# First weight unit and a norm row moved to the ACT queue, gate biases fetched once a branch, last rows finished by DVE in halves

## The chip, the cores and the metric

The kernel runs on one core of a Trainium2 chip. The metric is the device time of one execution in microseconds (us), the median of several runs. Five engines work side by side, each through its own list of instructions in order: TensorE (PE, matmuls and transposes), VectorE (DVE), ScalarE (ACT), GpSimd (POOL) and SyncE (SP), which here only issues transfers. They wait for each other, and for transfers, through semaphores. Data lies in HBM, in the on-chip memory SBUF (128 partitions) and, as results of PE, in PSUM.

## What is computed

Two layers of a hybrid block, then one layer of a second kind, over 256 tokens of width 1024, all in float32. Cut to the parts that the change touches:

```
def hybrid_layer(x, mem, ...):                      # twice
    h = rms_norm(x, ln_mix);  z = h @ w_in          # w_in: 1024 x 6440
    k, v = split(rms_norm(mem, mem_norm) @ mem_w_kv)   # memory attention's keys and values
    ...                                             # three attention branches o_nsa, o_gla, o_mem
    gates = sigmoid(merge.reshape(B, S, 3, D) + b_merge)   # merge: the last 3072 columns of z
    merged = sum(gates[:, :, i] * (o_i @ w_branch[i]))
    x = x + merged @ w_out
    h = rms_norm(x, ln_mlp)
    return x + square(relu(h @ w_up)) @ w_down
...
def hybrid_layer_2(x, ...):                         # once, the end of the program
    ...
    out = mixed @ w_out
    return layer_norm(ALPHA * x + out, ln_g, ln_b)  # (y - mean) * rsqrt(var + eps) * g + b
```

## The kernel before, in words

**Numbers.** Every float32 factor is split into a high part and the rest (`hi` and `lo` for weights, `b8x`, `hh`/`hl`, `oh`/`ol` for activations), and each product is three matmuls (`mm3`, line 188 records them all): high by high, rest by high, high by rest.

**Weights.** `unit` (line 434) loads 128 x 1024 elements (512 KB) into one of four buffers `raw` by a transfer of SP, ACT (every sixth time POOL) rounds them to `hi` (line 431, or 429 on POOL), and DVE takes the difference `lo` (line 432). The next transfer into a buffer waits until its `lo` is done. The very first unit is `fine`: its two halves of 128 x 512 are loaded and split each by itself (lines 442, 444, 445).

**The start.** PE first multiplies zeros (`warm`, line 324). SP loads the identity matrix (`CF`), the left half of the memory's 256 rows (`gate`, two tiles of 128 rows, by 512 columns), the row of `mem_norm` (into `ROWA`, called `gtmp` in the trace), the first half unit of `mem_w_kv`, and the right half of the memory. PE turns `ROWA` (line 192), DVE copies the column (`COL`), PE turns the memory's chunks of 128 columns, and ACT and DVE scale them into `b8x` high and rest (lines 524, 525). The keys' product follows (8 chunks k by 2 tiles of tokens), then the values' product, into which the turning of `X` is woven (4 transposes of a psm buffer each, three buffers), then layer 0. The rows of `ln_mix` and `ln_mlp` are loaded into other rows of the same `ROWA`; so that load waits for the first turning.

**Order of work.** PE's order is the order of the code. The others' lists are ordered by the scheduler of the framework, which follows dependencies. SP and ACT are in order: a transfer behind a waiting one is not issued. Transfers are counted on eight semaphores in turn, so the ninth transfer of a row waits until the first has landed, and so on.

**Gate biases.** `gates_of` (line 1120) makes the gates of a branch: a broadcast of 1024 numbers of `b_merge` to all partitions, twice (one copy for each tile of tokens, 1024 KB), fetched by POOL's queue into the buffer `gate`, then for each half of 512 columns DVE's `acc * rstd + bias` (line 1129) and ACT's tanh. For the first branch the buffer is free as soon as the memory's rows are used up.

**The end.** `fin` (line 1622) takes the last product: the last tile of tokens is computed in quarters of 256 columns, DVE adds the residual and gathers statistics; then the mean and variance (`bmv`, 1633), on POOL variance + eps (`bve`, 1635) and the power -0.5 (`brs`, 1637), on DVE the centering (1640) in pieces of 256 and 768 columns; then 256 columns are scaled by ACT (1644) and shifted by POOL (1645), 768 are done by DVE in one operation (1647), and SP writes the two pieces out (1648), the one of 256 first.

Of the kernel before, what the change touches and what calls it, by code (L numbers as in the profile page):

```python
# [19 lines left out]
P = 128  # L20
# [8 lines left out]
WARM = 8  # L29
WARM2 = 8  # L30
NRAW = 4
# [67 lines left out]
def block_kernel(ctx, tc, x_in, mem_in, positions, ln_mix, w_in, b_merge, nsa_q_norm, nsa_k_norm,  # L99
# [22 lines left out]
    def nm(s):  # L122
        cnt[0] += 1
        return f"{s}_{cnt[0]}"
# [113 lines left out]

    def load_mem(parts=(0, 1), mid=None, m=None):
        if m is None:  # L240
            m = B8("gate", shape=(2, 1024))
        for hf in parts:
            for tt in range(2):
                hs = slice(512 * hf, 512 * hf + 512)
                nc.sync.dma_start(m[:, tt, hs], mem_in[0, tt * P:(tt + 1) * P, hs])
            if mid is not None:
                mid()
        return m
# [9 lines left out]

    def first_rows():
        nc.sync.dma_start(ROWA[32:48, :], mem_norm.rearrange("l (k p) -> (l k) p", p=P))  # L260

    def ln_rows():
        nc.sync.dma_start(ROWA[0:16, :], ln_mix.rearrange("l (k p) -> (l k) p", p=P))
        nc.sync.dma_start(ROWA[16:32, :], ln_mlp.rearrange("l (k p) -> (l k) p", p=P))

    MEM0 = load_mem((0,), first_rows)

    def load_x():
        mem_stats()
        for tt in range(2):  # L270
            nc.sync.dma_start(X[:, tt], x_in[0, tt * P:(tt + 1) * P, :])
# [55 lines left out]
    pt = PS()  # L327
    tr(pt[:, :128], ROWA, IDF)
    dve.tensor_copy(COL[:, 32:48], pt[:, 32:48])
# [104 lines left out]
    def unit(srcs, a, n, fine=False):  # L434
        raw = wraw.tile([P, 1024], F32, tag="raw", name=nm("raw"))
        hi = whl.tile([P, 1024], FR, tag="hi", name=nm("hi"))
        lo = whl.tile([P, 1024], FR, tag="lo", name=nm("lo"))
        rv = raw[:, :a * n].rearrange("p (a n) -> p a n", a=a)
        if fine:
            (pp, c0, c1, src), = srcs  # L440
            for j in range(a):
                nc.sync.dma_start(rv[:, j], src[:, j])
                js = slice(j * n, j * n + n)
                act(hi[:, js], raw[:, js], AF.Copy)  # L444
                dve.tensor_tensor(lo[:, js], raw[:, js], f32(hi[:, js]), op=OP.subtract)
                if j == 0 and fine is not True:
                    fine()
            return (hi[:, :a * n].rearrange("p (a n) -> p a n", a=a),
                    lo[:, :a * n].rearrange("p (a n) -> p a n", a=a))
        for pp, c0, c1, src in srcs:  # L450
            nc.sync.dma_start(rv[pp, :, c0:c1], src)
        split(hi[:, :a * n], lo[:, :a * n], raw[:, :a * n])
        return (hi[:, :a * n].rearrange("p (a n) -> p a n", a=a),
                lo[:, :a * n].rearrange("p (a n) -> p a n", a=a))

    def units(w2d, r0, nk, cols, paired=None, fine=False):
# [14 lines left out]
        while k < nk:  # L471
            a = min(per, nk - k)
            rs = w2d[r0 + k * P:r0 + (k + a) * P, :]
            srcs = []
            o = 0
            for c0, c1 in cols:
                srcs.append((slice(0, P), o, o + c1 - c0, rs[:, c0:c1].rearrange("(a p) n -> p a n", p=P)))
                o += c1 - c0
            h, lo = unit(srcs, a, n, fine)
            fine = fine if fine is True and k < 2 else False  # L480
            for j in range(a):
                res.append((h[:, j, :], lo[:, j, :]))
            k += a
# [118 lines left out]
    def mem_kv(l, mh, ml, mid=None):  # L602
        w = mem_w_kv[l]
        pk = tok_major(mh, ml, w, 0, 8, [(0, 512)], l == 0 and (lambda: (load_mem((1,), None, MEM0), ln_rows())))
        if mid is not None:
# [513 lines left out]

    def gates_of(l, b, hh, hl, rsd):  # L1120
        g = B8("gate", shape=(2, 1024))
        nc.gpsimd.dma_start(g, wrap(b_merge[l, b], [[0, P], [0, 2], [1, 1024]]))
        for h in range(2):
            hs = slice(512 * h, 512 * h + 512)
            c0 = 3368 + 1024 * b + 512 * h
            ps = tok_major(hh, hl, w_in[l], 0, 8, [(c0, c0 + 512)])
            for tt in range(2):
                gs = g[:, tt, hs]
                dve.scalar_tensor_tensor(gs, ps[tt], rsd[:, tt:tt + 1], gs, op0=OP.mult, op1=OP.add)
                act(gs, gs, AF.Tanh, scale=0.5)  # L1130
# [71 lines left out]
    def layer(l, hT):  # L1202
# [85 lines left out]
        for b in (2, 1, 0):  # L1288
            g = gates_of(l, b, hh, hl, rsd)
            if b == 2:  # L1290
# [100 lines left out]
    def layer_2(hT):  # L1391
# [229 lines left out]
        def fin(tt, h, ps):  # L1621
# [12 lines left out]
            ve = SM([P, 1], "bve")  # L1634
            pool.tensor_scalar(ve, mv[:, 1:2], LN_EPS, None, op0=OP.add)
            rs = SM([P, 1], "brs")
            pool.tensor_tensor(rs, ve, MH[:, 0:1], op=OP.pow)  # L1637
            cuts = (slice(0, 256), slice(256, 1024))
            for qs in cuts:
                dve.scalar_tensor_tensor(X[:, tt, qs], X[:, tt, qs], mv[:, 0:1], LG[:, 0, qs],  # L1640
                                         op0=OP.subtract, op1=OP.mult)
            for q, qs in enumerate(cuts):
                if q == 0:
                    act(X[:, tt, qs], X[:, tt, qs], AF.Copy, scale=rs)
                    pool.tensor_tensor(X[:, tt, qs], X[:, tt, qs], LG[:, 1, qs], op=OP.add)
                else:
                    dve.scalar_tensor_tensor(X[:, tt, qs], X[:, tt, qs], rs, LG[:, 1, qs], op0=OP.mult, op1=OP.add)
                nc.sync.dma_start(out[0, tt * P:(tt + 1) * P, qs], X[:, tt, qs])
# [47 lines left out]
```

## Time and profile before

| | us |
|---|---|
| median of 3 runs (1228.67, 1231.71, 1232.16) | 1231.71 |
| the profiled execution | 1227.59 |
| its span, first to last instruction | 1225.8 |
| PE busy in the span | 1200.9 (98%) |
| DVE, ACT, POOL busy | 852.6, 583.1, 213.7 |

A busy share is the time in which an engine had an instruction in hand; PE's weight loads run beside its matmuls and have a row of their own. The 1.8 us between the profiled execution and its span lie outside the instructions. Idle time of an engine has in brackets, behind the instruction that ended it, what that instruction had waited for. In 24.9 us of the span PE does nothing, and most of that lies in three places: the first 39 us, the chunks of the gated linear attention in both layers (from 143 us and from 614 us on), and the end.

### The profile page before, as it was taken

What the parts mean: (1) busy time and instruction counts of PE and PEld (TensorE: products, weight loads), DVE (VectorE), ACT (ScalarE), POOL (GpSimd) and SP (SyncE); (2) the same over time, 40 slices, a digit from 0 to 9 for tenths busy, and PEclk for the clock granted to TensorE, in tenths of its full rate; (3) what the DMA queues carried; (4) which work ended last, traced back from release to release, by engine and by line L of the source; (5) the groups of instructions that cost most, each with busy time, mean ns of one, the idle gap of its engine ahead of it and who ended that gap; (6) DMA issues with size and microseconds to landing.
All of it is one profiled execution on the core that took longest, in us unless ns stands there. A gap on an engine that the chain in (4) does not pass through costs nothing. (4 is left out here: it accounts for less than half of the span.)

```text
span 1225.8 us, 18640 instructions
## 1 busy us (share of the span) xinstructions
PE 1200.9 (98%) x7069; PEld 1028.4 (84%) x7069; DVE 852.6 (70%) x1389; ACT 583.1 (48%) x926; POOL 213.7 (17%) x236
## 2 busy tenths in 40 slices
PE   8999999999999999999999999999999999999997
PEld 5787677888899899888777888999988997998876
DVE  5867988667654545668878767654554799985676
ACT  6566644444644434456655334543443334443351
POOL 2210220120111212210221030121121111000202
PEclk9999999999999999999999999999999999999998
DMA  8566523786656665656723676566566555466561
GB/s 296 179 174 179 170 87 108 220 224 213 200 188 185 190 190 177 188 160 164 202 66 114 198 209 200 167 193 194 183 189 195 178 178 164 139 186 192 172 207 67
DMA packets 139469, 217.10 MB, mean 177 GB/s; under 512 B 12145, under 2 KB 77013, under 8 KB 139380
## 3 DMA queue, kind: packets, MB, share of 16 engines
q1 hardware_dynamic: 137460, 209.47, 57.0%
q0 software_dynamic: 1920, 6.46, 1.8%
q8 instruction: 55, 0.90, 0.3%
q14 instruction: 34, 0.28, 0.1%
HBM read 215.01 MB, written 1.05 MB: 176 GB/s over the span
## 5 line engine op out<-in xcount | busy, mean ns | idle before, releaser
L432 DVE TENSOR_TENSOR lo<-raw,hi 128x1024 fp32r<-128x1024 f32 (+1 forms) x369 | 462.2, 1257 | 259.3 <-ACT hi L431 213.1
L431 ACT ACTIVATE hi<-raw 128x1024 fp32r<-128x1024 f32 (+1 forms) x308 | 324.6, 1058 | 428.2 <-PE acc L188 284.0
L188 PE MATMUL acc<-hi,hh 128*128 128x512 f32 (+1 forms) x512 | 205.7, 402 | 0.0
L188 PE MATMUL acc<-hi,hl 128*128 128x512 f32 (+1 forms) x512 | 197.1, 385 | 0.0
L188 PE MATMUL acc<-lo,hh 128*128 128x512 f32 (+1 forms) x512 | 196.7, 384 | 0.0
L429 POOL TENSOR_SCALAR hi<-raw 128x1024 fp32r<-128x1024 f32 x61 | 78.0, 1278 | 613.8 <-PE acc L188 476.5
L188 PE MATMUL acc<-hi,oh 128*128 128x512 f32 x400 | 157.9, 395 | 0.0
L188 PE MATMUL acc<-lo,oh 128*128 128x512 f32 x400 | 155.9, 390 | 0.0
L188 PE MATMUL acc<-hi,ol 128*128 128x512 f32 x400 | 155.9, 390 | 0.0
L188 PE MATMUL psm<-hh,hi 128*128 128x256 f32 x448 | 126.8, 283 | 0.0
L188 PE MATMUL psm<-hh,lo 128*128 128x256 f32 x448 | 126.8, 283 | 0.0
L188 PE MATMUL psm<-hl,hi 128*128 128x256 f32 x448 | 126.8, 283 | 0.0
L188 PEld LDWEIGHTS acc<-hi,hh 128*128 128x128 f32 x512 | 96.4, 188 | 20.4 <-issue 4.0
L188 PEld LDWEIGHTS acc<-hi,hl 128*128 128x128 f32 x512 | 96.1, 188 | 19.4
L188 PE MATMUL acc<-hh,hi 128*128 128x256 f32 x384 | 111.8, 291 | 0.0
L188 PEld LDWEIGHTS acc<-lo,hh 128*128 128x128 f32 x512 | 96.5, 188 | 16.3
L188 PE MATMUL acc<-hh,lo 128*128 128x256 f32 x384 | 108.7, 283 | 0.2 <-DVE lo L432 0.2
L188 PE MATMUL acc<-hi,b8x 128*128 128x512 f32 (+1 forms) x336 | 105.4, 386 | 3.6 <-ACT hi L444 2.1
L188 PE MATMUL acc<-hl,hi 128*128 128x256 f32 x384 | 108.8, 283 | 0.0
L188 PEld LDWEIGHTS acc<-hi,ol 128*128 128x128 f32 x400 | 75.1, 188 | 15.8
L188 PEld LDWEIGHTS acc<-hi,oh 128*128 128x128 f32 x400 | 75.2, 188 | 14.8
L188 PEld LDWEIGHTS acc<-lo,oh 128*128 128x128 f32 x400 | 75.2, 188 | 14.5
(362 smaller groups left out, 1869.5 us busy)
## 6 DMA issues: line engine op xcount, KB each, us to landing
raw<-in_w_in SPq DMA_DIRECT2D x160, 512.0 KB
raw<-in_w_up SPq DMA_DIRECT2D x64, 512.0 KB
raw<-in_w_down SPq DMA_DIRECT2D x64, 512.0 KB
raw<-in_w_branch SPq DMA_DIRECT2D x28, 512.0 KB
raw<-in_w_out SPq DMA_DIRECT2D x24, 512.0 KB
raw<-in_cmp_w SPq DMA_DIRECT2D x32, 256.0 KB
raw<-in_mem_w_kv SPq DMA_DIRECT2D x15, 512.0 KB
gate<-in_b_merge POOLq DMA_DIRECT2D x6, 1024.0 KB, 7.6
```

The lines of the kernel that those rows point to most:

```text
L188: nc.tensor.matmul(o, l, r, start=start, stop=stop, skip_group_check=True)
L429: pool.tensor_scalar(hi, raw, 1.0, 1.0, op0=OP.mult, op1=OP.mult)
L431: act(hi, raw, AF.Copy)
L432: dve.tensor_tensor(lo, raw, f32(hi), op=OP.subtract)
```

## The change

- The row of `mem_norm` gets a tile of its own (`ROWM`) and comes through ACT's queue.
- The first unit of `mem_w_kv` (`RAW0`) is asked for at the top: the first half by ACT's queue, as ACT's first instruction, the second by SP behind the memory's left half. `fine` then only splits.
- The memory's right half is asked for behind the second unit, the rows of `ln_mix` and `ln_mlp` just ahead of `X`.
- The second batch of `warm` has 4 matmuls and not 8.
- `b_merge` is fetched once a branch (512 KB): both tiles of tokens read the copy in `g[:, 0]`, tile 1 first, since tile 0 overwrites it. For the first branch of each layer a POOL copy of one column of `LOW` into the buffer stands ahead of the fetch, so that it can't start before `LOW` exists.
- At the end DVE adds eps, both pieces have 512 columns, and DVE does all of them.

```diff
-WARM2 = 8
+WARM2 = 4
...
-    def first_rows():
-        nc.sync.dma_start(ROWA[32:48, :], mem_norm.rearrange("l (k p) -> (l k) p", p=P))
-
+    ROWM = T2("tmp", (128,))
+    pool.memset(ROWM, 0.0)
+    nc.scalar.dma_start(ROWM[32:48, :], mem_norm.rearrange("l (k p) -> (l k) p", p=P))
...
-    MEM0 = load_mem((0,), first_rows)
+    MEM0 = load_mem((0,))
+    RAW0 = wraw.tile([P, 1024], F32, tag="raw", name="RAW0")
+    for j, q in enumerate((nc.scalar, nc.sync)):
+        q.dma_start(RAW0[:, 512 * j:512 * j + 512], mem_w_kv[0, j * P:j * P + P, 0:512])
 
     def load_x():
+        ln_rows()
         mem_stats()
...
-    tr(pt[:, :128], ROWA, IDF)
+    tr(pt[:, :128], ROWM, IDF)
...
-        raw = wraw.tile([P, 1024], F32, tag="raw", name=nm("raw"))
+        raw = RAW0 if fine else wraw.tile([P, 1024], F32, tag="raw", name=nm("raw"))
...
             for j in range(a):
-                nc.sync.dma_start(rv[:, j], src[:, j])
                 js = slice(j * n, j * n + n)
...
-            h, lo = unit(srcs, a, n, fine)
-            fine = fine if fine is True and k < 2 else False
+            h, lo = unit(srcs, a, n, fine and k == 0)
+            if fine and k == per:
+                fine()
...
-        pk = tok_major(mh, ml, w, 0, 8, [(0, 512)], l == 0 and (lambda: (load_mem((1,), None, MEM0), ln_rows())))
+        pk = tok_major(mh, ml, w, 0, 8, [(0, 512)], l == 0 and (lambda: load_mem((1,), MEM0)))
...
+        if after is not None:
+            pool.tensor_copy(g[:, 0, 0:1], after)
-        nc.gpsimd.dma_start(g, wrap(b_merge[l, b], [[0, P], [0, 2], [1, 1024]]))
+        nc.gpsimd.dma_start(g[:, 0], wrap(b_merge[l, b], [[0, P], [1, 1024]]))
...
-            for tt in range(2):
+            for tt in (1, 0):
                 gs = g[:, tt, hs]
-                dve.scalar_tensor_tensor(gs, ps[tt], rsd[:, tt:tt + 1], gs, op0=OP.mult, op1=OP.add)
+                dve.scalar_tensor_tensor(gs, ps[tt], rsd[:, tt:tt + 1], g[:, 0, hs], op0=OP.mult, op1=OP.add)
...
-            g = gates_of(l, b, hh, hl, rsd)
+            g = gates_of(l, b, hh, hl, rsd, LOW[:, 0, 0:1] if b == 2 else None)
...
-            pool.tensor_scalar(ve, mv[:, 1:2], LN_EPS, None, op0=OP.add)
+            dve.tensor_scalar(ve, mv[:, 1:2], LN_EPS, None, op0=OP.add)
...
-            cuts = (slice(0, 256), slice(256, 1024))
+            cuts = (slice(0, 512), slice(512, 1024))
...
-                if q == 0:
-                    act(X[:, tt, qs], X[:, tt, qs], AF.Copy, scale=rs)
-                    pool.tensor_tensor(X[:, tt, qs], X[:, tt, qs], LG[:, 1, qs], op=OP.add)
-                else:
-                    dve.scalar_tensor_tensor(X[:, tt, qs], X[:, tt, qs], rs, LG[:, 1, qs], op0=OP.mult, op1=OP.add)
+                dve.scalar_tensor_tensor(X[:, tt, qs], X[:, tt, qs], rs, LG[:, 1, qs], op0=OP.mult, op1=OP.add)
```

Three places show how instructions move. The first is SP's list at the top of the program, behind the memory's left half, before the change (`gate` is the memory, `gtmp` the tile of norm rows, `raw_136` the first unit; in brackets the semaphores waited for, `DMAHW` those of earlier transfers):

```order
L260 DMA gtmp_84<-in_mem_norm 16x128 [waits Pool_49]
L442 DMA raw_136<-in_mem_w_kv 128x512
L245 DMA gate_90<-in_mem 128x512 x2
L263 DMA gtmp_84<-in_ln_mix 16x128 [waits PE_49]
L264 DMA gtmp_84<-in_ln_mlp 16x128 [waits DMAHW0_49]
L442 DMA raw_136<-in_mem_w_kv 128x512 [waits DMAHW1_49]
L451 DMA raw_149<-in_mem_w_kv 128x2x512 [waits DMAHW2_49]
L451 DMA raw_155<-in_mem_w_kv 128x2x512 [waits DMAHW3_49]
```

and with it, from the memory's left half on:

```order
L245 DMA gate_93<-in_mem 128x512 x2
L267 DMA RAW_96<-in_mem_w_kv 128x512
L449 DMA raw_147<-in_mem_w_kv 128x2x512
L245 DMA gate_93<-in_mem 128x512
L245 DMA gate_93<-in_mem 128x512 [waits DMAHW0_49]
L449 DMA raw_155<-in_mem_w_kv 128x2x512 [waits DMAHW1_49]
L449 DMA raw_161<-in_mem_w_kv 128x2x512 [waits DMAHW2_49]
L261 DMA gtmp_84<-in_ln_mix 16x128 [waits DMAHW3_49,Pool_49]
```

The second half of the first unit stands third and not eighth, ahead of every wait; the memory's last quarter now waits for `DMAHW0`, which counts the half unit on ACT's queue.

The second is ACT's list there, before (`hi_137` is the first unit, `hi_150` the second, `b8x_132` the memory's high parts, one chunk a row, from the transposes `psm_167`, `_188` and so on):

```order
L524 ACTIVATE b8x_132<-psm_167,COL 128x256 [waits DVE_49,PE_49]
L444 ACTIVATE hi_137<-raw_136 128x512 [waits DMAHW4_49]
L524 ACTIVATE b8x_132<-psm_167,COL 128x256 [waits DVE_49]
L524 ACTIVATE b8x_132<-psm_188,COL 128x256 [waits PE_49]
L444 ACTIVATE hi_137<-raw_136 128x512 [waits DMAHW1_49]
L524 ACTIVATE b8x_132<-psm_188,COL 128x256 [waits DVE_49]
L524 ACTIVATE b8x_132<-psm_200,COL 128x256 [waits PE_49]
L431 ACTIVATE hi_150<-raw_149 128x1024 [waits DMAHW2_49]
```

and with it (`RAW_96` is the first unit, `hi_148` the second; `gate_93` in the last row is the square of the memory's rows):

```order
L267 DMA RAW_96<-in_mem_w_kv 128x512
L259 DMA tmp_90<-in_mem_norm 16x128 [waits Pool_49]
L444 ACTIVATE hi_141<-RAW_96 128x512 [waits DMAHW0_49]
L523 ACTIVATE b8x_137<-psm_167,COL 128x256 [waits DVE_49,PE_49]
L444 ACTIVATE hi_141<-RAW_96 128x512 [waits DMAHW5_49]
L523 ACTIVATE b8x_137<-psm_167,COL 128x256 [waits DVE_49]
L433 ACTIVATE hi_148<-raw_147 128x1024 [waits DMAHW6_49]
L523 ACTIVATE b8x_137<-psm_184,COL 128x256 [waits PE_49]
L523 ACTIVATE b8x_137<-psm_196,COL 128x256 [waits PE_49]
L564 ACTIVATE gate_93,mssq_258<-gate_93 128x1024 [waits DMAHW7_49,DMAHW2_49,PE_49]
```

The second unit's rounding now stands ahead of the copies of chunks 2 to 4, and the copies' order is 0, 1, 2, 4.

The third is DVE's list at the very end, for the last tile of tokens, before:

```order
L1626 SCALAR_TENSOR_TENSOR X<-X,acc_11832 128x256
L1630 BN_STATS fst_11737<-X 128x6
L1633 BN_AGGR bmv_11859<-fst_11737 128x2
L1640 SCALAR_TENSOR_TENSOR X<-X,bmv_11859,hh_11641 128x256
L1640 SCALAR_TENSOR_TENSOR X<-X,bmv_11859,hh_11641 128x768
L1647 SCALAR_TENSOR_TENSOR X<-X,brs_11863,hh_11641 128x768
```

and with it:

```order
L1627 SCALAR_TENSOR_TENSOR X<-X,acc_11831 128x256
L1631 BN_STATS fst_11737<-X 128x6
L1634 BN_AGGR bmv_11858<-fst_11737 128x2
L1636 TENSOR_SCALAR bve_11860<-bmv_11858 128x1
L1641 SCALAR_TENSOR_TENSOR X<-X,bmv_11858,hh_11641 128x512 x2
L1644 SCALAR_TENSOR_TENSOR X<-X,brs_11862,hh_11641 128x512 x2
```

One small operation is added ahead of the centering, and the last operation is now two of 512 columns (`x2`), with no work of ACT or POOL behind the power.

## Rows read from the trace of the kernel before

**Rows 1.** Busy time of each engine in three stretches (the columns are named in the first line; behind each busy time the number of instructions; PEclk is the granted clock of PE as a share of full speed).

```profile
core 0: us, PE busy (x) PEld busy (x) DVE busy (x) ACT busy (x) POOL busy (x), PEclk, DMA share, GB/s
0.00:39.00 39.00, 31.82 (x146) 23.10 (x147) 23.55 (x44) 24.70 (x42) 7.55 (x22) 1.00 0.75 253
39.00:1217.30 1178.30, 1169.12 (x6925) 1005.34 (x6923) 825.47 (x1339) 557.89 (x884) 203.48 (x211) 1.00 0.59 175
1217.30:1225.80 8.50, 0.00 (x0) 0.00 (x0) 3.55 (x6) 0.51 (x1) 2.72 (x3) 0.61 0.33 123
```

**Rows 2.** PE's instructions at the start, in order of time: start us, duration, engine, line, what is written from what, count; in brackets the idle time ahead of it and what ended it.

```profile
5.08 0.30 PE L192 MATMUL psm<-CF,gtmp 128*128 128x128 f32 x1 [0.60 <-DMA gtmp<-in_mem_norm]
5.22 0.60 PE L192 MATMUL psm<-CF,gate 128*128 128x128 f32 x4
5.66 1.89 PE L324 MATMUL acc<-WZ 128*128 128x512 bf16 x8
7.20 0.58 PE L188 MATMUL acc<-hi,b8x 128*128 128x512 f32 x1
9.34 0.60 PE L192 MATMUL psm<-CF,gate 128*128 128x128 f32 x4
12.02 0.50 PE L188 MATMUL acc<-hi,b8x 128*128 128x512 f32 x1 [2.08 <-ACT hi L444]
12.74 0.50 PE L188 MATMUL acc<-lo,b8x 128*128 128x512 f32 x1 [0.22 <-DVE lo L445]
...
33.13 0.63 PE L192 MATMUL psm<-CF,X 128*128 128x128 f32 x4 [2.92 <-DVE kss L579]
```

**Rows 3.** Transfers issued by SP at the start: start us, time in which the issues lie, target and source, count.

```profile
1.17 0.89 SPq L245 DMA_DIRECT2D gate<-in_mem  x2
2.11 0.43 SPq L260 DMA_DIRECT2D gtmp<-in_mem_norm  x1
2.58 0.42 SPq L442 DMA_DIRECT2D raw<-in_mem_w_kv  x1
3.04 0.91 SPq L245 DMA_DIRECT2D gate<-in_mem  x2
5.42 0.33 SPq L263 DMA_DIRECT2D gtmp<-in_ln_mix  x1
6.26 0.42 SPq L442 DMA_DIRECT2D raw<-in_mem_w_kv  x1
6.72 1.46 SPq L451 DMA_DIRECT2D raw<-in_mem_w_kv  x3
...
23.09 5.42 SPq L451 DMA_DIRECT2D raw<-in_w_in  x4
```

**Rows 4.** ACT's instructions at the start, in the same columns as rows 2.

```profile
5.86 0.47 ACT L524 ACTIVATE b8x<-psm,COL 128x256 fp32r<-128x256 f32 x1 [3.64 <-PE psm L192]
...
11.33 0.63 ACT L444 ACTIVATE hi<-raw 128x512 fp32r<-128x512 f32 x1 [2.02 <-DMA raw<-in_mem_w_kv]
12.66 1.06 ACT L431 ACTIVATE hi<-raw 128x1024 fp32r<-128x1024 f32 x1
...
24.95 1.05 ACT L431 ACTIVATE hi<-raw 128x1024 fp32r<-128x1024 f32 x1
29.10 1.06 ACT L431 ACTIVATE hi<-raw 128x1024 fp32r<-128x1024 f32 x1 [3.10 <-DMA raw<-in_w_in]
```

**Rows 5.** The gate bias of the first branch: its issue by POOL; the line of the six such fetches in the view of transfers (KB each as read and written, median us from issue to landing); two stretches in the columns of rows 1; and the first write of `LOW` in layer 0.

```profile
19.61 0.79 POOL L1122 DMA_DIRECT2D gate<-in_b_merge  x1 [0.46 <-issue]
...
gate<-in_b_merge POOLq DMA_DIRECT2D x6, 1024.0 KB, 7.6
...
23.00:30.00 7.00, 7.00 (x39) 5.64 (x37) 5.34 (x7) 3.90 (x6) 1.18 (x2) 1.00 0.92 332
88.00:96.00 8.00, 8.00 (x65) 7.24 (x63) 7.70 (x24) 3.30 (x7) 0.00 (x0) 1.00 0.15 39
...
85.29 0.28 ACT L1254 ACTIVATE LOW<-acc,xrs 128x16 f32<-128x16 f32 x1
```

**Rows 6.** The end: what follows the last statistics, in order of time; SP's last two issues; DVE's mean for a piece of 512 columns (count, busy us, mean ns, idle us before); and one DVE operation on 8 columns.

```profile
1218.23 0.26 DVE L1633 BATCH_NORM_AGGREGATE bmv<-fst 128x2 f32<-128x24 f32 x1
1218.53 1.42 DVE L1640 SCALAR_TENSOR_TENSOR X<-X,bmv,hh 128x256 f32<-128x256 f32 x2
1218.58 0.51 POOL L1635 TENSOR_SCALAR bve<-bmv 128x1 f32<-128x1 f32 x1 [1.72 <-DVE bmv L1633]
1219.18 1.19 POOL L1637 TENSOR_TENSOR brs<-bve,MH 128x1 f32<-128x1 f32 x1
1220.41 0.51 ACT L1644 ACTIVATE X<-X,brs 128x256 f32<-128x256 f32 x1 [4.65 <-POOL brs L1637]
1220.41 1.02 DVE L1647 SCALAR_TENSOR_TENSOR X<-X,brs,hh 128x768 f32<-128x768 f32 x1 [0.46 <-POOL brs L1637]
1220.99 1.01 POOL L1645 TENSOR_TENSOR X<-X,hh 128x256 f32<-128x256 f32 x1 [0.62 <-ACT X L1644]
...
1222.03 0.81 SPq L1648 DMA_DIRECT2D out<-X  x2
...
L1626 DVE SCALAR_TENSOR_TENSOR X<-X,acc 128x512 f32<-128x512 f32 x3 | 2.0, 684 | 2.2 <-PE acc L188 2.2
...
32.90 0.16 DVE L579 TENSOR_SCALAR kss<-kss 128x8 f32<-128x8 f32 x1
```

More of the change, by code (lines that the diff above doesn't have):

```diff
@@ L237, in block_kernel, with load_mem @@
     CF = consts.tile([P, CO_END], F32, name="CF")
-    def load_mem(parts=(0, 1), mid=None, m=None):
+    def load_mem(parts=(0, 1), m=None):
         if m is None:
@@ L245, in load_mem @@
                 nc.sync.dma_start(m[:, tt, hs], mem_in[0, tt * P:(tt + 1) * P, hs])
-            if mid is not None:
-                mid()
         return m
@@ L439, in unit @@
         if fine:
-            (pp, c0, c1, src), = srcs
             for j in range(a):
-                nc.sync.dma_start(rv[:, j], src[:, j])
                 js = slice(j * n, j * n + n)
@@ L445, in unit @@
                 dve.tensor_tensor(lo[:, js], raw[:, js], f32(hi[:, js]), op=OP.subtract)
-                if j == 0 and fine is not True:
-                    fine()
             return (hi[:, :a * n].rearrange("p (a n) -> p a n", a=a),
@@ L1118, in row_bcast, with gates_of @@
         return rb
-    def gates_of(l, b, hh, hl, rsd):
+    def gates_of(l, b, hh, hl, rsd, after):
         g = B8("gate", shape=(2, 1024))
-        nc.gpsimd.dma_start(g, wrap(b_merge[l, b], [[0, P], [0, 2], [1, 1024]]))
+        if after is not None:
+            pool.tensor_copy(g[:, 0, 0:1], after)
+        nc.gpsimd.dma_start(g[:, 0], wrap(b_merge[l, b], [[0, P], [1, 1024]]))
         for h in range(2):
```

## The prediction

> **What bounds the kernel now.** I read the busy times by stretch first [rows 1]. From 39 us to 1217.3 us PE works 1169.12 of 1178.30 us: no other engine and no transfer sets the time there, and what the change moves in that stretch is worth at most parts of the 9.2 us left. PE idles 7.2 us in the first 39 and all 8.5 us of the end. So the change is worth what it takes out of these two. The granted clock of PE is full (2.4 GHz) at the start and in the middle [rows 1]; no term comes from it.
>
> PE's own waits at the start come second [rows 2]: 0.60 us for the row of `mem_norm`, 2.08 and 0.22 us for the second half of the first weight unit, and 2.92 us ahead of the last turning of `X`. Third, who caused them. SP had to wait with the `ln_mix` row until 5.42, because the tile is turned at 5.08, and the second half unit stood behind that row: issued at 6.26 [rows 3], landed at 11.33 [rows 4], while PE was ready at about 9.9. The 2.92 us start with ACT, which sits from 26.0 to 29.10 at the rounding of the first `w_in` unit [rows 4]; the copies that free a psm buffer stand behind it. That unit was issued at 23.09 [rows 3] and took 6.0 us, beside 1024 KB of gate bias issued at 19.61 [rows 5].
>
> **Part by part.**
>
> *First matmul.* The turning of the memory began at 5.22, the first product at 7.20, when the 8 warming matmuls (1.89 us, 0.236 us each) were through [rows 2]. Four fewer are 0.94 us. But 256 KB more now compete with the memory's left half, from the ACT queue: at the 253 GB/s of this stretch [rows 1] that is 1.0 us if all of it goes first, 0 if it goes last; I take 0.5. The copy began 0.64 us behind the turning (5.22 to 5.86 [rows 2, 4]) and takes 0.47; with turning at 5.7 the first product starts at 6.9: gain 0.3. Bounds: -0.5 (turning 1.0 late, 6.22 + 0.64 + 0.47 = 7.33, and the copy of the rest some 0.4 behind it) and +0.9. The row of `mem_norm` comes earlier, which alone is worth nothing, since the memory's tiles are behind it.
>
> *The hole of 2.08 + 0.22 us* goes: the second half unit is issued behind the memory's left half, near 2.1 and not 6.26; with the 5.07 us it took it lands at 7.2, ahead of need. What is late next is the memory's right half. Its last quarter is issued only when the half unit on ACT's queue has landed, and the second unit (512 KB) stands ahead of both quarters. Up to it 64 + 8 + 1024 + 512 + 512 KB = 2.17 MB must move; with nothing moving before 2.0 and 300 GB/s from there (an estimate; the mean with the empty start is 253 [rows 1]) that is 9.2, and PE wants the chunks at 9.34 - 0.3 = 9.0. With some landing time I put a new hole of 0.7; bounds 0 and 3. Net 2.30 - 0.7 = 1.6.
>
> By the Trainium skill, "DMA: Bandwidth & Descriptors", section "Queues, rings and completion order", one issuer's descriptors are taken in order on each DMA engine. By that rule the second half unit, issued at 6.26 into a nearly empty queue, would have been down near 9 us and the old hole next to nothing. The row says 11.33: 5.07 us for 256 KB, as if it shared with the 2.5 MB issued behind it. So I let the measurement decide; by the rule the new hole would be near 0 and the whole sum 5.2.
>
> *ACT between.* From 12.66 to 26.0 ACT has no gap (17 rows from the first to the last, none with a wait [rows 4]), so it, not PE, paces how early the values' units are rounded. Its list starts earlier, with the second unit, issued near 2.6 instead of 6.72 [rows 3]; but that rounding now stands ahead of the copies of chunks 2 to 4, so a late unit holds the copies up. I take 0.3 off for that; bounds 0 and 2.
>
> *The hole of 2.92 us.* The 1024 KB bias leaves this stretch: at 332 GB/s [rows 5] it is 1.05 MB / 0.332 = 3.2 us of transfer time, so the `w_in` unit could land near 26, where ACT becomes free. But PE now comes 0.3 + 1.6 - 0.3 = 1.6 us earlier, while that unit's issue is released by ACT's and DVE's pace, perhaps 0.8 earlier. In place, 2.92 + 1.6 - 0.8 - 3.1 leaves about 0.6; with the new order of copies I leave 1.0. Gain 1.9; bounds 0.5 and 2.9.
>
> Start: 0.3 + 1.6 - 0.3 + 1.9 = 3.5 us.
>
> *Gate biases elsewhere: 0.* Three MB fewer are read as written, in a stretch where PE does not wait. The first fetch now waits for `LOW` (85.29 us) and falls into 88 to 96 us, where the transfers' share is 0.15 [rows 5]; behind the waiting POOL copy stands only the rounding of a unit not yet loaded. If that cover were gone, 512 KB would cost 0.524 / 0.332 = 1.6 us a layer. DVE's swapped tiles and the later tanh have a whole product's time until the same accumulator is wanted.
>
> *The end.* Variance + eps: POOL started 0.09 us behind the statistics and took 0.51 [rows 6]; DVE does it for about 0.16. The power starts at 1218.75 instead of 1219.18, ends at 1219.95. DVE's two centerings (2 x 0.684) end near 1220.05, and the last two pieces at 1220.75 and 1221.4. Before, the piece through ACT and POOL ended at 1222.00, and SP, in order, issued both pieces at 1222.03 to 1222.84 [rows 6]. Now the issues end at about 1221.8, and the first half leaves 1.2 us earlier: 1.0 us; bounds 0.7 and 1.4. DVE's extra 0.2 us for the first tile of tokens is covered by its wait for the last quarter's product.
>
> Sum: 3.5 + 1.0 = 4.5 us of 1227.59, so 1223.1 for an execution like the profiled one. The median of the runs shown is 4.1 us above that execution, and the lowest of them 1.1; what makes the runs differ no row shows. I put the change under the median: 1231.71 - 4.5 = 1227.2.
>
> **Rivals.**
>
> *A: ACT paces the start, the holes only move.* For: 13.3 us without a gap, nearly the same list of work. Against: the list starts up to 3 us earlier, and its first gap, 26.0 to 29.10, was a transfer's. The last hole closes by its lower bound, 0.5, and ACT's order costs 0.9: 0.3 + 1.6 - 0.9 + 0.5 = 1.5 at the start, 2.5 in all: 1229.2.
>
> *B: slower. SP is held by the half unit on ACT's queue.* SP issues nothing behind the memory's third quarter until that half has landed. At 5.07 us from issue it lands at 5.8 and nothing is lost; the price starts when the last quarter lands behind 12.0, where PE went on before. If the half took twice as long, 10.1 us (landing 10.9), the last quarter, issued then and 2.9 us under way like the small row (2.11 to 5.05 [rows 2, 3]), would land at 13.8. The keys then go on 1.8 late; the third unit, issued at 11.3 instead of about 7.2, adds some 2; the 2.92 us stay; the end gives 1.0 back: 2.8 slower, 1234.5. Against: the queue is nearly empty when that half is asked for.
>
> *C: the bias was not what held the `w_in` unit.* Then that unit still takes 6.0 us, the 2.92 us hole grows by what PE gains before it less 0.8, and the start gives 0.8, with the end 1.8: 1229.9. For: three more `w_in` units share the queue with it. Against: the 3.2 us fit the 3.10 us that ACT waited.
>
> By the skill's same page, section "Issuing engines are not separate DMA queues", a second issuer saves only the time to initiate. Here that would be the 0.42 us of one issue [rows 3]. What the kernel loses at 5.42, though, is order: the half unit stands behind a wait, and the change takes it from there on SP's own list.
>
> **How the numbers follow.** Forecast (gain 2.7 or more at the start) 0.60; A 0.18; C 0.12; B 0.07; 0.03 for a small loss elsewhere. A difference of 0.3% (3.7 us) is about what a measurement of this kernel can tell from no change. Of the forecast all but 0.03 lies beyond it; A, C and the small loss lie within it, and of B 0.04 beyond it on the other side. So faster 0.57, same 0.39, slower 0.04. All upper bounds at once are 0.9 + 2.3 + 2.9 + 1.4 = 7.5 us; with 6.7 under a run like the lowest (1228.67) the lower end is 1222.0. The upper end takes in A and C, 1.8 and 2.5, under the highest run (1232.16), and smaller gains down to 0.7: 1231.5.
>
> **What would show it.** Right: no wait for `RAW0` at the second chunk; the first product at 6.5 to 7.3; a wait for the memory's right half under 1.5 us; the `w_in` rounding at 25 to 27; the last turning of `X` at 29 to 30.5 instead of 33.13; DVE's last piece 1.0 us or more before the old end. Wrong: PE waiting for a turned chunk of the right half beyond 11 us; ACT without a gap up to the copies of `X`; the first `w_in` unit still 6 us under way; a new PE wait near 90 us or 560 us.

## The result, and the profile after

The change makes the kernel 0.6% faster: 1224.18 us (median of 4 runs, 1222.39 to 1225.60) against 1231.93 (4 runs, 1228.67 to 1233.29) measured beside it; the ratio is 0.9942, 95% interval 0.9919 to 0.9964. The later runs give the size better: 16 runs of the changed kernel (those 4 and 12 later ones) have a mean of 1225.89 us, 100 runs of the kernel before, made beside the experiments on four chips, 1230.86, so 4.97 us less. One more run of the kernel before, 1697.97 us at a mean granted clock of 0.653, was in the slow state and is left out. The profiled execution took 1224.30 (span 1222.5), only 3.3 us under the one profiled before; why that is less than the runs say is the main thing that this case teaches.

Busy time of the changed kernel in the three stretches of [rows 1], cut at the end of PE's last matmul:

```profile
core 0: us, PE busy (x) PEld busy (x) DVE busy (x) ACT busy (x) POOL busy (x), PEclk, DMA share, GB/s
0.00:39.00 39.00, 36.78 (x158) 27.21 (x159) 24.93 (x47) 28.30 (x45) 7.18 (x22) 1.00 0.72 237
39.00:1215.40 1176.40, 1167.16 (x6908) 1003.03 (x6907) 823.99 (x1339) 555.07 (x879) 204.09 (x212) 1.00 0.57 173
1215.40:1222.50 7.10, 0.01 (x1) 0.00 (x0) 3.91 (x8) 0.00 (x0) 0.98 (x1) 0.71 0.27 101
```

PE's idle time in the first 39 us fell from 7.18 to 2.22 us [rows 1], and the end is shorter. PE at the start, columns as in [rows 2]:

```profile
4.96 0.45 PE L192 MATMUL psm<-CF,tmp 128*128 128x128 f32 x1 [0.18 <-DMA tmp<-in_mem_norm]
5.20 0.46 PE L192 MATMUL psm<-CF,gate 128*128 128x128 f32 x1
5.87 0.90 PE L192 MATMUL psm<-CF,gate 128*128 128x128 f32 x3 [0.21 <-DMA gate<-in_mem]
6.57 1.91 PE L326 MATMUL acc<-WZ 128*128 128x512 bf16 x4
7.92 0.99 PE L188 MATMUL acc<-hi,b8x 128*128 128x512 f32 x1
8.71 0.63 PE L188 MATMUL acc<-lo,b8x 128*128 128x512 f32 x1
10.20 0.48 PE L188 MATMUL acc<-hi,b8x 128*128 128x512 f32 x1
...
29.47 0.63 PE L192 MATMUL psm<-CF,X 128*128 128x128 f32 x4 [0.45 <-DVE hl L524]
```

The waits of 2.08 and 0.22 us for the second half unit are gone, and the last turning of `X` comes at 29.47, not 33.13 [rows 2]. But the 4 warming matmuls took 1.91 us, where 8 had taken 1.89: up to about 9.9 us PE ran at half its rate, 0.45 us for 512 columns and not 0.236. That is the ratio of the two levels of its clock, 1.2 and 2.4 GHz, but the column of the granted clock reads 1.00 in this stretch, so only the durations tell. ACT, where the first `w_in` unit had been waited for [rows 4]:

```profile
26.48 1.05 ACT L433 ACTIVATE hi<-raw 128x1024 fp32r<-128x1024 f32 x1
...
29.44 1.06 ACT L433 ACTIVATE hi<-raw 128x1024 fp32r<-128x1024 f32 x1 [0.61 <-DMA raw<-in_w_in]
```

The end, to be laid beside [rows 6] (the last row holds SP's four output transfers, the last of them issued up to 1219.82):

```profile
1216.36 0.26 DVE L1634 BATCH_NORM_AGGREGATE bmv<-fst 128x2 f32<-128x24 f32 x1
1216.66 0.15 DVE L1636 TENSOR_SCALAR bve<-bmv 128x1 f32<-128x1 f32 x1
1216.73 1.41 DVE L1641 SCALAR_TENSOR_TENSOR X<-X,bmv,hh 128x512 f32<-128x512 f32 x2
1216.89 0.98 POOL L1638 TENSOR_TENSOR brs<-bve,MH 128x1 f32<-128x1 f32 x1 [4.17 <-DVE bve L1636]
1218.05 1.41 DVE L1644 SCALAR_TENSOR_TENSOR X<-X,brs,hh 128x512 f32<-128x512 f32 x2
1213.67 6.15 SPq L1645 DMA_DIRECT2D out<-X  x4
```

So 3.66 us are gained up to the turning of `X`, and the end, from the start of PE's last matmul, takes 7.37 instead of 8.80 us (1215.13 to 1222.5; 1217.00 to 1225.8). Together 5.1; the spans differ by 3.3. I followed the lead of the changed kernel from PE instruction to PE instruction: 3.67 us up to 141 us, 3.37 to 560, 3.17 up to 630, and 1.67 from 637 on. Most of what is missing went in that one place. PE there, and windows of 2 us:

```profile
627.34 3.64 PE L188 MATMUL psm<-KB,b8x 128*128 128x16 f32 x32
630.84 0.76 PE L188 MATMUL psm<-MLR,T 128*128 128x512 f32 x2
632.80 1.55 PE L188 MATMUL pso<-pts,n 128*64 128x256 f32 x8
```

```profile
630.00:632.00 2.00, 2.00 (x13) 1.81 (x13) 0.91 (x3) 0.00 (x0) 0.00 (x0) 0.84 0.00 0
632.00:634.00 2.00, 2.00 (x11) 0.92 (x9) 1.77 (x9) 0.90 (x2) 0.00 (x0) 0.50 0.00 0
634.00:636.00 2.00, 2.00 (x11) 1.47 (x8) 0.30 (x2) 0.66 (x2) 0.07 (x1) 0.81 0.00 0
```

Behind a row of products of 16 columns (16 of them, 32 matmuls in the trace: the scores against the compressed keys, line 841, once a layer) the granted clock fell to 0.50, and PE lost 1.5 us without being idle. In the profile before the clock reads 1.00 there.

### The profile page after: what moved, and what is told of

Its sections match the earlier page's. It is cut to its first block, busy times and chain, and to the rows that moved or that the text cites. A ratio compares the mean times of both kernels' runs of the same rounds, so it can differ in the third digit from the quotient of the medians.

```text
span 1222.5 us, 18627 instructions
## 1 busy us (share of the span) xinstructions
PE 1203.9 (98%) x7065; PEld 1030.2 (84%) x7065; DVE 852.8 (70%) x1393; ACT 583.4 (48%) x924; POOL 212.3 (17%) x235
```

## The experiments

All kernels below were compared with the kernel before on the same chip; means are over the runs given. "Up" is the time up to which PE's matmuls at the start have the long durations, "X" the last turning of `X`, "end" the stretch from PE's last matmul to the end of the span, "fall" where the granted clock fell in the profile of that kernel; all in us.

| kernel | first product | up | X | end | fall at | mean (runs) | mean clock |
|---|---|---|---|---|---|---|---|
| before | 7.20 | 5.1 | 33.13 | 8.80 | none | 1230.86 (100) | 0.9946 |
| changed | 7.92 | 9.9 | 29.47 | 7.37 | 630 | 1225.89 (16, with e8) | 0.9954 |
| e1_end | 9.88 | 9.9 | 33.87 | 7.36 | 35, 165 | 1229.66 (12) | 0.9952 |
| e2_bias | 9.84 | 9.8 | 32.01 | 8.78 | none | 1227.30 (10) | 0.9959 |
| e3_start | 7.98 | 9.9 | 29.65 | 8.83 | 631 | 1226.59 (8) | 0.9961 |
| e7_early | 8.15 | 9.5 | 29.77 | 7.40 | 160 | 1226.05 (7) | 0.9959 |
| e8_after | 6.78 | 4.6 | 29.32 | 7.39 | 160 | 1226.49 (12) | 0.9949 |
| e4_warm8 | 8.20 | 5.2 | 30.40 | 7.39 | 633 | 1226.86 (12) | 0.9954 |
| e5_warm10 | 7.83 | 7 | 30.14 | 7.32 | 161 | 1225.06 (8) | 0.9964 |
| e9_memfirst | 8.33 | 7.2 | 29.70 | 7.34 | 160, 633 | 1226.32 (12) | 0.9952 |
| e6_spread | 7.03 | 6.3 | 29.24 | 7.39 | 690 | 1230.55 (12) | 0.9974 |
| e10_cut2 | 7.99 | 9.6 | 29.50 | 7.34 | none | 1226.07 (12) | 0.9982 |
| e11_fill | 7.32 | 6.2 | 29.82 | 7.35 | 160 | 1225.70 (12) | 0.9962 |
| e12_late | 7.30 | 4.7 | 29.62 | 7.37 | none | 1228.23 (12) | 0.9981 |

**The end alone** (before, with the last three hunks of the change):

```diff
-            pool.tensor_scalar(ve, mv[:, 1:2], LN_EPS, None, op0=OP.add)
+            dve.tensor_scalar(ve, mv[:, 1:2], LN_EPS, None, op0=OP.add)
...
-            cuts = (slice(0, 256), slice(256, 1024))
+            cuts = (slice(0, 512), slice(512, 1024))
...
```

> The kernel before with the edit of the end alone (DVE adds eps, two pieces of 512 columns, DVE finishes both). In the profile with the whole change the time from PE's last matmul to the end of the span fell from 8.52 to 7.09 us. If that is the edit's own, the same stretch falls by 1.3 to 1.5 us here, and everything ahead of PE's last matmul stays as before; the time falls by about 1.4 us (ratio 0.9989). If the prediction's 1.0 us were right, the stretch is 7.5. Rival: the medians of before and after differ by 7.2 us where the profiled spans differ by 3.3, so something that the profile of one execution does not show moves the times; if it hangs on the end, this kernel gains more than 2 us.

Ratio 0.9987 (0.9972 to 1.0002). The time alone does not show it; the end stretch does, 7.36 us, the same to 0.05 in every kernel with this edit, and 8.78 to 8.83 in every kernel without. It is worth 1.44 us. The rival falls. More telling is the rest of this profile, since its start is the start of before. PE, then two windows:

```profile
5.73 0.45 PE L192 MATMUL psm<-CF,gtmp 128*128 128x128 f32 x1 [0.95 <-DMA gtmp<-in_mem_norm]
5.97 1.06 PE L192 MATMUL psm<-CF,gate 128*128 128x128 f32 x4
6.82 3.62 PE L324 MATMUL acc<-WZ 128*128 128x512 bf16 x8
9.88 0.91 PE L188 MATMUL acc<-hi,b8x 128*128 128x512 f32 x1
...
13.50 0.50 PE L188 MATMUL acc<-lo,b8x 128*128 128x512 f32 x1 [0.23 <-DVE lo L445]
...
33.87 0.63 PE L192 MATMUL psm<-CF,X 128*128 128x128 f32 x4 [2.83 <-DVE kss L579]
```

```profile
34.00:36.00 2.00, 2.00 (x9) 1.60 (x9) 1.97 (x4) 1.09 (x3) 0.00 (x0) 0.61 0.02 4
36.00:38.00 2.00, 2.00 (x7) 1.57 (x6) 1.81 (x10) 0.47 (x1) 0.00 (x0) 0.53 0.09 3
```

With unchanged code the 8 warming matmuls took 3.62 us here and 1.89 in [rows 2], the first product came at 9.88 instead of 7.20, and of the waits for the second half unit, which had landed meanwhile, 0.23 us for its `lo` were left. The 2.83 us ahead of `X` are there all the same, and here the clock fell behind them: PE, 0.73 us behind the kernel before at `X`, was 2.3 behind at 39 us, 1.6 us more.

**The bias alone, the start alone, and the whole change with the bias fetched early.** Edits: in the first, only `gates_of` and its call change; in the second everything ahead of the values' product, nothing of `gates_of` and the end; in the third the hold is taken off:

```diff
-            g = gates_of(l, b, hh, hl, rsd, LOW[:, 0, 0:1] if b == 2 else None)
+            g = gates_of(l, b, hh, hl, rsd, None)
```

> The kernel before with the gate biases fetched once a branch and, for the first branch, after LOW; start and end as before. Theory: the 1024 KB of bias held the first w_in unit (6.0 us from issue to use). Then ACT rounds that unit at 26 to 27.5 instead of 29.10, the idle time of 2.92 us ahead of the last turning of X falls under 1.2, that turning comes near 31, and 1.7 to 2.9 us are gained. Rival C of the prediction: the bias did not hold that unit; the rounding stays at 28.5 to 29.1, the turning at 33, and nothing is gained. Second rival: the later fetch costs a wait of PE behind 85 us or 555 us; then the lead at 39 us is lost again there.

> The change of the start alone (first unit, memory's norm row, order of the right half, four warming matmuls fewer); 1024 KB of bias still fetched early, the end as before. Theory: the keys are through 1.7 us earlier as with the whole change (values' first product near 21.5 instead of 23.15), but the first w_in unit still shares the queue with the bias, so the last turning of X comes at 32 to 33 and only 0 to 1.2 us are left at 39 us: time 0 to 1.2 us less. Rival C: the bias plays no part; then the last turning comes near 29.5 as with the whole change and 3.4 to 3.7 us are gained.

> The whole change, but the first branch's bias (512 KB now) is not held back until LOW exists, so it is fetched near 19 us again. Theory: half the bias costs about half of what the whole cost: the first w_in unit is rounded 0.8 to 1.6 us later than with the whole change (26.48), the last turning at 30 to 31 instead of 29.47; the time is 0.7 to 1.6 us above the changed kernel's. Rival C: no difference, the turning at 29.5 and the rounding at 26.5. In either case the end is as with the change (7.1 us behind PE's last matmul).

Ratios 0.9970 (0.9955 to 0.9986), 0.9967 (0.9949 to 0.9984) and 0.9958 (0.9941 to 0.9974). PE ahead of the last turning of `X`, in e2_bias and then in e3_start:

```profile
32.01 0.63 PE L192 MATMUL psm<-CF,X 128*128 128x128 f32 x4 [1.32 <-DVE kss L579]
```

```profile
29.65 0.52 PE L192 MATMUL psm<-CF,X 128*128 128x128 f32 x3 [0.56 <-DVE hl L524]
```

and the rounding of the first `w_in` unit on ACT, in the same order:

```profile
27.18 1.06 ACT L431 ACTIVATE hi<-raw 128x1024 fp32r<-128x1024 f32 x1 [0.74 <-DMA raw<-in_w_in]
```

```profile
26.79 1.06 ACT L433 ACTIVATE hi<-raw 128x1024 fp32r<-128x1024 f32 x1
```

(The last of the four turnings lies outside the stretch shown for e3_start.) My theory said that the bias held that unit. Alone, with the old start, it does: the unit is rounded 3.64 us after its issue and not 6.01, and the hole is 1.32 us and not 2.83 (e1_end has the same start). But with the new start the full 1024 KB, fetched as early as 18.39, do no harm: ACT finds the unit there, the hole is 0.56, and `X` comes 0.18 later than with the whole change. Rival C's figure was right for the start alone and the theory's 0 to 1.2 us wrong. e7_early says the same: `X` at 29.77, 0.3 us later, where the theory had 30 to 31. Part of the gains in the means is the clock: e2_bias is 3.5 us faster than the kernel before and only 1.12 us ahead at `X`, and its mean clock is higher by 0.0013. The two edits close one hole, each nearly alone; their gains don't add. A likely cause, argued and not tried alone, is that the new start asks for the values' units 2.2 us earlier (at 10.48 and not 12.71), so that less is under way when the `w_in` units are asked for.

**The change again.** No edit.

> The changed kernel once more, unaltered, for more runs and a second profile. Over 24 runs of the kernel before, the time goes with the mean granted clock of the run (about 1.2 us for each 0.001), and the mean clock is 0.9946; the 4 runs of the changed kernel had 0.9968. Theory: at an equal clock the change is worth 4 us, and the rest of the 6.7 us between the means is fewer falls of the clock; then these runs have a mean clock of 0.996 to 0.997 and a mean of 1223.5 to 1225. Rival: the 4 runs were lucky and the clock falls as often as before; then the mean clock is 0.995 and the mean 1226 to 1227.

Mean 1226.49 at a mean clock of 0.9949, ratio 0.9967 (0.9951 to 0.9982): the rival on the clock is right, the four first runs were lucky. The changed kernel's clock falls about as often as before. Its start in this profile:

```profile
6.05 1.03 PE L326 MATMUL acc<-WZ 128*128 128x512 bf16 x4
6.78 0.53 PE L188 MATMUL acc<-hi,b8x 128*128 128x512 f32 x1
...
10.27 0.30 PE L192 MATMUL psm<-CF,gate 128*128 128x128 f32 x1 [1.34 <-DMA gate<-in_mem]
10.86 0.55 PE L192 MATMUL psm<-CF,gate 128*128 128x128 f32 x3 [0.29 <-DMA gate<-in_mem]
```

Same code, but PE had the short durations from 4.6 us on: the first product comes 1.14 us earlier, and now PE does wait for the memory's right half, 1.63 us. The last turning of `X` is at 29.32, only 0.15 earlier. The head start goes in that one wait: it is 2.2 us just ahead of it, 0.24 behind it and 0.16 from there to `X`.

**Warming.** `WARM2` 4 to 8, and `WARM` 8 to 10, in the changed kernel.

> The changed kernel with 8 warming matmuls in the second batch, as before. In the changed kernel's profile the 4 took 0.48 us each, that is 1.2 GHz, and the first product began at 7.92. Theory: the clock rises at 9.5 to 10 whatever PE is given ahead of it, so 4 more cost 1.7 to 1.9 us at the first product (9.6 to 9.8), of which about 1.2 come back since the first chunk then runs at 2.4 GHz; the last turning of X comes 0.3 to 0.8 later than 29.47. Rival: the first batch's successors decide, and 8 warm the clock up by 6 us as in the profile of before; then each takes 0.24, the first product begins near 8.5 and runs at full speed, and nothing is lost.

> The changed kernel with 10 warming matmuls ahead of the norm row and not 8. They fill the 0.18 and 0.21 us in which PE waits for the row and for the memory's first rows. Theory: those gaps do not decide when the clock rises; the first chunk runs at 1.2 GHz up to 9.5 to 10, the first product begins at 7.9 to 8.3, and the last turning stays within 0.4 us of 29.47. Rival: it is the idle gaps that keep the clock down; without them it rises near 5.5, the second batch takes 0.24 us each, the first product begins near 7.1 and the first three chunks are through 1.5 to 2 us earlier.

Ratios 0.9958 (0.9939 to 0.9978) and 0.9956 (0.9940 to 0.9973): neither differs from the changed kernel. In the profile of the first PE had the short durations from 5.2 us on and the 8 took 1.89, as the rival had it; in that of the second from near 7. With e8_after (4.6) against the changed kernel's first profile (9.9) on identical code, neither the count of matmuls nor the two short waits explain when the rate rises. Both theories are unsupported; what sets it stays open. The last turning came at 30.40 and 30.14, later than either theory allowed: the hole ahead of it, waiting for DVE's `hl`, was 1.18 and 0.91 us and not 0.45; the cause is open.

**The memory's right half ahead of the second unit** (changed kernel):

```diff
         q.dma_start(RAW0[:, 512 * j:512 * j + 512], mem_w_kv[0, j * P:j * P + P, 0:512])
+    load_mem((1,), MEM0)
...
-        pk = tok_major(mh, ml, w, 0, 8, [(0, 512)], l == 0 and (lambda: load_mem((1,), MEM0)))
+        pk = tok_major(mh, ml, w, 0, 8, [(0, 512)], l == 0 and (lambda: None))
```

> The changed kernel with the memory's right half issued ahead of the second weight unit. In the second profile of the changed kernel PE's clock was up early, the first product began at 6.78, and PE then waited 1.34 and 0.29 us for that right half (chunks turned at 10.27 and 10.86); the last turning of X came at 29.32 all the same, as in the profile with the slow clock (29.47). Theory: that hole is real but nothing ends there, since ACT and the next units set the pace up to X; the right half comes 1 to 1.6 us earlier, the hole moves to the second unit (PE or ACT waits for it near 11 to 12), and the last turning stays within 0.4 us of 29.4. Rival: the hole is what holds the start; then the last turning comes at 28.2 or earlier and a microsecond is gained.

Ratio 0.9965 (0.9945 to 0.9985), nothing gained, as the theory said, if not for its reason. The hole behind the second chunk goes; PE waits elsewhere:

```profile
7.22 0.55 PE L192 MATMUL psm<-CF,gate 128*128 128x128 f32 x3 [1.86 <-DMA gate<-in_mem]
...
13.59 0.50 PE L188 MATMUL acc<-lo,b8x 128*128 128x512 f32 x1 [0.62 <-DVE lo L435]
...
29.70 0.52 PE L192 MATMUL psm<-CF,X 128*128 128x128 f32 x3 [0.75 <-DVE hl L525]
```

The left half, whose issues stand ahead in either kernel, was there at 5.87 and is there at 7.22; the second unit is rounded at 11.23 and not 9.28, and PE waits 0.62 us for its `lo`. `X` stays at 29.70: what one transfer gains by coming earlier, the others lose. That ACT sets the pace here, as the theory had it, is not shown.

**The row of small products.** In four groups of 4 (e6_spread), in two of 8 (e10_cut2), with products whose result nobody reads behind groups of 4 (e11_fill), and in two of 8 with the following steps due later (e12_late). A `yield` lets other work of PE go ahead; its number is the due time of what follows, in ns. The names behind `#` tell whose lines these are:

```diff
                 mm(pcv[:, tt, 16 * h:16 * h + 16], QS[:, h, tt * P:tt * P + P], KB[:, h % 2, :], True, True)
+                if h % 4 == 3 and (tt, h) != (1, 7):      # e6_spread
+                    yield 300.0
...
+            if tt == 0:                                   # e10_cut2, e12_late
+                yield 300.0
...
+                if h % 4 == 3 and (tt, h) != (1, 7):      # e11_fill
+                    for _ in range(2):
+                        mm(pc[:, 256:512], IDB, CBT[:, 0:256], True, True)
...
-        yield 7050.0                                      # e12_late
+        yield 9050.0
...
-        yield 800.0                                       # e12_late
+        yield 1200.0
```

> The changed kernel with the 16 products of 16 columns (all heads' scores against the compressed keys, once a layer) cut into four groups of 4 with other work of PE between them. In the changed kernel's profile the granted clock fell to 0.50 behind that row of small products at 630 us, and 1.5 us were lost; in two other profiles it fell at the same place of a layer, at 160 or 630. Theory: the falls come from that row, in which PE streams few columns; spread out, no profile shows a fall there, the mean granted clock of the runs is 0.998 and the mean time 1 to 2 us under the changed kernel's on the same chip. Rival: the falls come at random times wherever PE waits, and nothing changes; or the spreading costs PE as much in waits on DVE as it saves.

> The changed kernel with the 16 products of 16 columns cut into two groups of 8, one piece of other work of PE between them. Cut into four groups the mean granted clock rose from 0.9949 to 0.9974, but the scores came so late that PE waited 2 to 3 us a layer for what follows, and the time was 4 us above the changed kernel's. Theory: with one cut the delay is a third and stays without a wait, while the clock falls less often: mean clock 0.996 or more, mean time 1 to 2 us under the changed kernel's (1226.5 on the chip of the last runs; 4.5 us under before). Rival: 8 in a row are enough for the clock to fall, and the mean stays at 0.995; or the delayed scores make PE wait again, and the time is above the changed kernel's.

> The changed kernel with two products of 256 columns in bf16, whose result nobody reads, behind each of the first three groups of 4 of those 16 small products: the order of all other work stays, and PE is given 6 x 0.11 = 0.7 us more a layer, 1.3 us in all. Theory: it is the small products that let the clock fall; with columns in between it falls less often, the mean clock rises to 0.997, that is 2.4 us by the slope of 1.2 us for each 0.001, and 1 us is left: 5.5 to 6 us under before. Rival: the fall is set by something else there (the waits of PE of 0.8 us just ahead of it); then the clock stays at 0.995 and the time is 1.3 us above the changed kernel's.

> As the kernel with the small products in two groups of 8, but the due time of what follows the scores (turning of the weighted scores) 2.0 us later, and that of their use 0.4 later, so that other work of PE stands ahead of the two waits of 1.56 and 0.72 us that the cut had brought. Two groups of 8 gave a mean clock of 0.9982 and twelve runs within 2.1 us of each other, but a mean as the changed kernel's, 1226.1. Theory: the clock stays as high and the waits go: mean 1223.5 to 1224.5, 1.5 to 2.5 us under the changed kernel's, 6 to 7 us under the kernel before's. Rival: DVE is the one that is late there, and another wait of PE on DVE takes the place; then the mean stays near 1226.

Ratios 1.0009 (0.9995 to 1.0023), 0.9964 (0.9952 to 0.9977), 0.9960 (0.9946 to 0.9974) and 0.9980 (0.9968 to 0.9991). In the ten profiles with the row whole the clock fell behind it 9 times in 20 passes (two layers each); in the three with the row cut, never in 6. The same place in e10_cut2:

```profile
156.00:160.00 4.00, 4.00 (x31) 3.33 (x32) 1.59 (x4) 2.34 (x10) 0.00 (x0) 1.00 0.34 125
160.00:164.00 4.00, 4.00 (x32) 3.46 (x27) 1.62 (x7) 0.98 (x2) 0.40 (x1) 1.00 0.00 0
...
629.00:633.00 4.00, 4.00 (x32) 3.56 (x30) 1.59 (x4) 2.44 (x10) 0.00 (x0) 1.00 0.46 131
633.00:637.00 4.00, 4.00 (x30) 3.32 (x30) 1.05 (x6) 0.65 (x2) 0.00 (x0) 1.00 0.02 4
```

None of the 36 runs of the cut kernels has a clock under 0.996, of the changed kernel's 16 half have. That cutting the row keeps the clock up is shown. PE's waits just ahead do not explain the falls: those of 0.31 and 0.81 us ahead of the second layer's row (620 to 627 us) stand in e10_cut2 with 0.31 and 0.82, and no fall follows. That it is the small products themselves, and not the order of the work around them, is not shown: e11_fill keeps the order and puts columns between, and one fall remains. No time came of the cuts, because the scores are late and PE waits for what follows (e10_cut2, then e12_late):

```profile
171.74 0.41 PE L192 MATMUL psm<-CF,n 128*128 128x128 f32 x2 [1.56 <-DVE n L865]
...
644.46 0.41 PE L192 MATMUL psm<-CF,n 128*128 128x128 f32 x2 [0.72 <-DVE n L865]
```

```profile
170.98 0.68 PE L188 MATMUL psm<-QB,b8x 128*128 128x128 f32 x4 [1.18 <-DVE QB L1042]
```

With other work put ahead PE waits on DVE a step on: the last rival's mechanism holds, DVE is the late one, and the mean of 1228.23 is 2 us above the 1226 that it gave. e6_spread, with waits of 1.1 us at the same step in both layers and of 1.11 and 1.88 further on, is over 4 us slower than the changed kernel. Only the evenness stays: the runs of e10_cut2 lie within 2.1 us of each other and those of e12_late within 2.9, those of the changed kernel within 7.0. The filling products did not keep the clock up (one fall in two passes) and gained nothing that can be told.

## Why the prediction was right

**The sum.** Predicted were 4.5 us, start 3.5 and end 1.0; the means give 4.97. In the profiles it is 3.66 at `X` and 1.43 at the end, less what the clock took behind. Of the 4.97 about 0.9 is a clock higher by 0.0008 (0.9954 to 0.9946, at the slope below), so at an equal clock the change is worth about 4.1 us. The medians shown first differ by 7.75: that surplus was luck, four runs at a mean clock of 0.9968, where the 12 later ones had 0.9949. The forecast of 1227.2 was 3.0 us above the measured median mostly for the same reason. The 1 us between 5.1 and 4.1 is not fully explained; in the profile 0.3 us went at 143 us and 0.2 us from 575 us on.

**The base.** I made the sum under the median of the runs, not under the profiled execution, without knowing what made the runs differ. It goes with PE's clock, to which the prediction gave no term. Over the 100 runs of before a mean clock lower by 0.001 goes with 1.1 us (correlation -0.88), from 1225.8 at 0.998 to 1237.4 at 0.989. The execution profiled before had the short durations from 5.1 us on and no fall; it lies 3.3 us under the mean. The changed kernel's had one fall, worth 1.5 us. That is why the two profiled spans differ by less than the runs.

**First matmul.** Forecast 6.9, bounds 6.3 to 7.7; measured 6.78 and 7.92, the second outside. The step "four fewer are 0.94 us" took 0.236 us for one as a property of the kernel. It is that of one execution: 0.45 in others.

**The hole for the second half unit** went, as forecast. But its 2.30 us, too, were those of one execution: in e1_end and e2_bias, with the old start and long durations up to 9.9 and 9.8 us, 0.23 were left without the change. The new one for the memory's right half, put at 0.7 with bounds 0 and 3, is 0 in one profile and 1.63 in the other, above the 1.5 that the prediction allowed for being right: it is there when PE is fast enough to reach it. So PE's rate and this hole offset each other: at 14 us PE is 1.66 us ahead of the kernel before in one profile and 1.82 in the other, where the terms up to here gave 1.9, though each of them was off by about a microsecond in one of the two. That the sum held is partly luck. I had cited the Trainium skill, "DMA: Bandwidth & Descriptors", section "Queues, rings and completion order", and read its order as putting this hole near 0; the 1.63 us speak against that reading, and so do e9_memfirst's 7.22 against 5.87 for transfers already issued.

**ACT between**, 0.3, was 0.46: of the 1.66 us at 14 us (1.82 in e8_after) 1.21 (1.36) are left at 23, lost at one product that waits for DVE's `lo`, and from there to the hole ahead of `X` PE has no wait. PE, then ACT in the changed kernel's first profile:

```profile
22.15 0.50 PE L188 MATMUL acc<-lo,b8x 128*128 128x512 f32 x1 [0.19 <-DVE lo L434]
...
26.10 0.48 ACT L523 ACTIVATE hh<-psm,COL 128x256 fp32r<-128x256 f32 x1 [0.83 <-PE psm L192]
```

Rival A's mechanism did not come: ACT now has gaps in which it waits for PE, the head start of e8_after went in a wait for a transfer and not in ACT's pace, and the hole at the end closed by 2.47 us and not by 0.5.

**The hole of 2.92 us.** Left were 0.45 and 0.46 instead of 1.0 (up to 1.18 in e4_warm8). The size was near; the reason was the step that failed. "The 1024 KB bias leaves this stretch" is enough with the old start (1.32 left) and not needed with the new one (0.56 left).

**Gate biases elsewhere: 0.** Confirmed: no new wait of PE near 90 or 560 us in the changed kernel's profiles. In those of e10_cut2 and e11_fill, whose code is the changed kernel's up to there, PE waits 0.74 and 0.70 us near 97 us, since ACT got a `w_in` unit late; the share of the transfers was 0.01 and 0.02 from 88 to 92 us there, so the bias was down by then, and what held that unit is open.

**The end**, 1.0 with bounds 0.7 and 1.4, was 1.43. The order of steps was right. The power took 0.98 us where 1.19 was taken over from before, which changed nothing, since DVE's centering ended later (1218.14, the power 1217.87). Counted from PE's last matmul, SP's issues end 1.15 us earlier, 1.04 by the forecast; the last transfer ended 2.68 us behind its issue instead of 2.96, for which there was no term (1222.5 less 1219.82, 1225.8 less 1222.84).

**Rival B** did not come: the half unit on ACT's queue was there at 4.49, and SP lost less than a microsecond.

## What to carry to other kernels

Before taking an execution as the base of a sum, compare durations of equal instructions in it (warming matmuls, for one) with a second profile: the same code gave 7.20 and 9.88 for its first product. Two edits that aim at one hole must be priced together, and once each; what the second adds is what the first leaves. Time won ahead of a wait for a transfer is lost in that wait: first products 1.14 us apart ended 0.15 apart at `X`, so look where the stage ends, not where it starts.

## What the runs showed of the hardware

PE's rate at the start rose at 4.6 us in one profile of the changed kernel and at 9.9 in another, with the same instructions ahead of it, while the granted clock in the windows read 1.00. Later in the program the granted clock fell to 0.50 for some microseconds while PE was busy all the time, behind 16 products of 16 columns; in e1_end and e6_spread also behind PE waits of 2.83 and 1.88 us. By PE's lead over the kernel before, six of the nine falls behind the whole row cost 1.5 us (one is the changed kernel's at 630 us) and three cost 3.1 us (one is that of e8_after at 160 us). The spread between runs goes with them: with the row cut in two the runs of a kernel agree within 2.1 and 2.9 us, those of the experiments with the row whole within 2.8 to 7.9 (7 to 12 runs each); e6_spread, which has a fall elsewhere, has 5.2.
